# Opening of a two-layer transformer block: order of the modulation chunks, of the first weight loads and splits, and of the rows of h

## The chip, the cores and the metric

The kernel runs on one core of one Trainium2 chip, in one launch. The metric is the device time in microseconds (us); a median over the runs shown is compared. The core has five engines that work side by side and wait for one another by semaphores: PE (TensorE, matmuls), DVE (VectorE), ACT (ScalarE), POOL (GpSimd) and SP (SyncE), which here issues the DMA transfers. Each engine works through its own instructions in order. Line numbers such as L195 are lines of the kernel before.

## What is computed

The reference runs two layers over a sequence x of 512 tokens and a context of 256 tokens, both 1024 wide. Only the start of layer 0 matters here: the modulation vectors, the normalised and modulated input h, and its product with the first projection's weights. The filter of the long convolution is computed beside it.

```python
def _rms_norm(x, g):
    y = x32 * lax.rsqrt(jnp.mean(x32 * x32, axis=-1, keepdims=True) + EPS)
    return (y * _f32(g)).astype(x.dtype)

def _adaln(cond, w_mod, b_mod):
    mod = jax.nn.silu(cond) @ w_mod + b_mod
    return jnp.split(mod[:, None, :], 6, axis=-1)

def _modulate(h, shift, scale):
    return h * (1 + scale) + shift
...
        sh1, sc1, g1, sh2, sc2, g2 = _adaln(c, w_mod[i], b_mod[i])
        hx = _modulate(_rms_norm(x, norm1[i]), sh1, sc1)
...
def _fourier_hyena_mixer(h, w_in, w_out, ...):
    proj = h @ w_in
...
    h = jnp.sin(f * (z @ _f32(w1) + _f32(b1)))
    h = jnp.sin(f * (h @ _f32(w2) + _f32(b2)))
    h = jnp.sin(f * (h @ _f32(w3) + _f32(b3)))
    h = h @ _f32(w4)
```

## The kernel before

Activations lie with the 1024 features on the partitions, as eight row tiles of 128 features by 772 columns: 512 columns of x, two of padding, 256 of the context, two of padding. "Row d of h" is such a tile.

Products of full precision are made from split operands. A float32 value is kept as a high part in a reduced format and a low part, the rest. For a weight tile `wr` of 128 by 1024, ACT makes the high part `wh` (L98) and DVE the low part `wl` (L103); `wsplit` makes both, `wraw` only issues the load (L111). For a row of h, `a1` and `a2` (for x and for the context) call `scaled`, which lets DVE multiply by the norm and the scale A (L266) and ACT add the shift and write the high part `hh` (L267), and `low`, which lets DVE write the low part `hl` (L271). `mm3` then issues three matmuls for each product: `wh` by `hh` (L123), `wh` by `hl` (L124), `wl` by `hh` (L125). `proj_k` does that for one row k and one weight tile m, for the 512 and for the 260 columns: six matmuls, called a block here. `first(m, k)` is such a block, for the first three output tiles m of the projection and the eight rows k.

The modulation of layer 0 that h needs, shift and scale, is a product of the two conditions with 2048 columns of `w_mod`. It is made in four chunks of 512 columns. A chunk's weights are two loads of 1 MB (L180, `gemv_raw`) into one of three buffers `wm`. `gemv_pe` issues the chunk's matmuls (L189), the copy of their sums out of PSUM on ACT (L192), the turn, four products of a 128 by 128 piece of that copy with a selector of two columns (L195), which put the result on the partitions, and the add of the bias on DVE (L200). After the fourth chunk DVE makes A (L218), and then h can begin.

Between the chunks stand two other pieces. The norm's statistic takes squares on ACT (L233), sums them on PE (L234), copies the sums (L244), puts them on the partitions (L248), computes 1/sqrt by small DVE operations (the last is L141), spreads it over the partitions on PE (L256) and copies it to SBUF (L259); it runs once for x and once for the context. The three layers of the filter's small network each are a product (L359), a chain of DVE operations that reduces the argument of the sine (L333 to L342), and the sine on ACT (L343). The product of its result with w4 (L372) is the first thing that PE does after the blocks. Chunks, turns, statistics and layers share two PSUM buffers called `ms`.

The order of PE, DVE, ACT and SP in the opening is written out by hand: inside `manual_schedule` each engine works in the order in which the program calls. POOL's order, and all that comes after, is planned by the framework. Eight loads can be under way on SP's queue, since each of eight semaphores is used again only when its last load has landed.

Of the kernel before, what the change touches and what calls it, by code (L numbers as in the profile page):

```python
# [14 lines left out]
ALU = mybir.AluOpType  # L15
# [3 lines left out]
P = 128  # L19
D = 1024  # L20
KD = 8
# [12 lines left out]
def _columns():  # L34
    names = [("n1_0", 8), ("n1_1", 8), ("n2_0", 8), ("n2_1", 8), ("bm_0", 48), ("bm_1", 48)]
    names += [(f"fcw{i}{k}", NF) for i in range(2) for k in range(3)]
    names += [(f"fcb{i}", NF) for i in range(2)]
    names += [(f"hcw{k}", 12) for k in range(3)] + [("hcb", 12)]
    names += [("fb1", 1), ("fb2", 1), ("fb3", 1), ("ffr", 1)]
    names += [("qan", 2), ("kvan", 1), ("qg", 2), ("kg", 2), ("kpg", 1)]  # L40
    off, o = {}, 0
    for n, w in names:
        off[n] = (o, w)
        o += w
    return off, o


COLS, NCOLS = _columns()


class Builder:
# [130 lines left out]

    def gemv_pe(self, i, chunk, raw):

        nc = self.nc
        ps = self.ms()
        for kt in range(KD):
            q = kt % 4
            nc.tensor.matmul(ps[32 * q : 32 * q + 32, :], self.sT[:, kt, :], raw[:, 512 * kt : 512 * kt + 512],  # L189
                             start=kt < 4, stop=kt >= 4, tile_position=(0, 32 * q))  # L190
        g = self.t(self.S2, [P, 512], F32, "s2")
        nc.scalar.copy(g, ps)  # L192
        pc = self.ms()
        for b in range(4):
            nc.tensor.matmul(pc[:, 2 * b : 2 * b + 2], g[:, 128 * b : 128 * b + 128], self.sel, start=True, stop=True)  # L195
        sec, d0 = ((0, 0), (1, 0), (0, 4), (1, 4))[chunk]
        jt = 8 * sec + d0
        o = COLS[f"bm_{i}"][0] + jt
        bm = self.pcol[:, o : o + 4].rearrange("p (a o) -> p a o", o=1).to_broadcast([P, 4, 2])
        nc.vector.tensor_tensor(self.mod[i][:, jt : jt + 4, :], pc[:, 0:8].rearrange("p (a b) -> p a b", b=2), bm, op=ALU.add)  # L200

    def gemv_dve(self, i, jt, conds=(0, 1)):

# [255 lines left out]
    def mixer(self):  # L459
        nc, I = self.nc, self.I  # L460
# [19 lines left out]
        with self.tc.manual_schedule(engines={ENG.PE, ENG.DVE, ENG.SP, ENG.Activation}):  # L480
            layer = self.filter_mlp()
            for d in range(KD):
                nc.sync.dma_start(x[d][:, 0:512], I["xT"][d])
            wm = [self.gemv_raw(0)]
            for d in range(KD):
                nc.sync.dma_start(x[d][:, C0 : C0 + C], I["cxT"][d])
            wm.append(self.gemv_raw(1))
            nc.sync.dma_start(self.w4, I["w4"])
            wm.append(self.gemv_raw(2))
            pa = layer(0, None, 0)  # L490
            for d in range(KD):
                s1(d)
            h = layer(0, pa, 1)
            f1(True, 0)
            pa = layer(1, h, 0)
            f1(True, 1)
            h = layer(1, pa, 1)
            self.gemv_pe(0, 0, wm[0])
            wm.append(self.gemv_raw(3))
            for tt in (4, 5):  # L500
                dec[tt] = tp()
                nc.sync.dma_start(dec[tt], I["decay"][tt])
            win = [self.wraw(I["w_in"][m]) for m in range(3)]
            for d in range(KD):
                s2(d)
            f2(True, 0)
            pa = layer(2, h, 0)
            f2(True, 1)
            self.gemv_pe(0, 1, wm[1])
            h3 = layer(2, pa, 1)  # L510
            self.gemv_pe(0, 2, wm[2])
            self.gemv_pe(0, 3, wm[3])
            self.make_A(0, 0)
            self.close("wm")
            hp = self.pool("hp", side="right")
            for d in range(KD):
                hh.append(self.t(hp, [P, TW], F32R, f"hh{d}"))
                hl.append(self.t(hp, [P, TW], F32R, f"hl{d}"))
            self.zero_pads(hh + hl)

            def both(d, step):
                a1(d, step)
                return a2(d, step)


            ps3, wins = [self.mm() for _ in range(3)], []

            def first(m, k):
                self.proj_k(ps3[m], wins[m], hh, hl, k)

            both(0, 0)
            wins.append(self.wsplit(win[0]))
            both(1, 0)
            both(0, 1)
            first(0, 0)
            wins.append(self.wsplit(win[1]))
            both(2, 0)
            both(1, 1)
            first(0, 1)
            first(1, 0)  # L540
            first(1, 1)
            wins.append(self.wsplit(win[2]))
            both(3, 0)
            both(2, 1)
            first(0, 2)
            first(1, 2)
            first(2, 0)
            first(2, 1)
            first(2, 2)
            for d in range(4, KD + 1):  # L550
                if d < KD:
                    last_act = both(d, 0)
                last = both(d - 1, 1)
                for m in range(3):
                    first(m, d - 1)
        self.dbg("h0", hh, hl)


# [68 lines left out]
        def turn(i, f):  # L627
            pt = self.mm()
            for k in range(6):
                nc.tensor.transpose(pt[:, 128 * k : 128 * k + 128], f[:, 128 * k : 128 * k + 128], self.ident)  # L630
            src = pt[:, 0:768].rearrange("p (a b) -> p a b", b=128)
            w = slice(128 * i, 128 * i + 128)
            self.hi(uTh[:, :, w], src)
            self.lo(uTl[:, :, w], src, uTh[:, :, w])
# [96 lines left out]
        for src, b, c, n in ((I["cs128"], csh[:], csl[:], 256), (I["fcos"], flat(cth), flat(ctl), 1040), (I["fsin"], flat(sth), flat(stl), 1024)):  # L731
            for o in range(0, n, 520):
                m = min(520, n - o)
# [706 lines left out]
```

## Time and profile before

| | us |
|---|---|
| runs, median (3 runs) | 1829.6 |
| runs, lowest and highest | 1828.78 and 1830.51 |
| the profiled execution, its own time | 1830.64 |
| its span, first to last instruction | 1828.8 |
| PE busy in the span | 1706.3 (93%) |
| DVE busy | 1022.0 (56%) |
| ACT busy | 613.9 (34%) |
| POOL busy | 121.3 (7%) |

Durations in the profile come from one execution. Matmuls are pipelined, and their ends are modelled, so two that overlap add up to less than the sum of their records. A busy share over the whole span says little about the opening, which is 5% of it; it has to be read in its own stretch. The granted clock is the share of full speed at which PE was allowed to run; its mean over the span is 0.958. In the views of the trace an arrow in brackets names what ended the idle time before an instruction.

### The profile page before, as it was taken

The numbers are of one execution on the slowest core, as the hardware profiler recorded it, in microseconds if no ns is written. First come the engines' busy times: TensorE is split into PE (matmuls) and PEld (weight loads), VectorE is DVE, ScalarE is ACT, GpSimd is POOL, SyncE is SP. The second block draws the span as 40 slices with busy tenths as digits, with TensorE's granted clock in tenths as the row PEclk, the third lists the DMA queues.
The fourth block names the chain that finished last, engine by engine and source line by source line (L and its number), as shares of the span: only waits on it lengthen the run. The fifth ranks groups of instructions, "written<-read, shape, count | busy, mean of one in ns | idle before, by whom it ended". The sixth has DMA issues, their size and how long they took to land.

```text
span 1828.8 us, 21719 instructions
## 1 busy us (share of the span) xinstructions
PE 1706.3 (93%) x8742; PEld 1326.3 (73%) x8742; DVE 1022.0 (56%) x1662; ACT 613.9 (34%) x830; POOL 121.3 (7%) x202
## 2 busy tenths in 40 slices
PE   6889975799899999999999887899998999999999
PEld 2657864787688888888888556555554777888887
DVE  3486966864898435543434554665764554444443
ACT  3332222323323212222122434655663443223231
POOL 0052113310000000000000000110110000000000
PEclk7799987899999999999999998899999999999999
DMA  9032520352355234431312310000002323322322
GB/s 351 24 127 71 171 78 30 103 173 81 116 174 176 88 104 140 147 128 70 121 47 85 117 60 24 1 12 12 12 12 70 116 72 101 104 93 92 104 75 98
DMA packets 53249, 172.83 MB, mean 95 GB/s; under 512 B 6043, under 2 KB 8925, under 8 KB 52125
## 3 DMA queue, kind: packets, MB, share of 16 engines
q1 hardware_dynamic: 53149, 171.45, 27.4%
q8 instruction: 69, 1.13, 0.2%
q14 instruction: 31, 0.25, 0.0%
HBM read 167.23 MB, written 4.19 MB: 94 GB/s over the span
## 4 chain that ended last, share of the span: by engine, by line
PE 77%; DVE 11%; ACT 5%; POOL 3%; issue 3%; DMA 1%; POOLq 0%; SPq 0%; ACTq 0%; DVEq 0%
PE mm L123 21%; PE mm L124 20%; PE mm L125 20%; PE pv L1176 2%; PE ms L234 2%; PE z L1164 2%; DVE junk L210 2%; DVE wl L103 1%; DVE S L1154 1%; PE s L1130 1%; ACT S L1145 1%; PE s L123 1%; PE s L124 1%; PE s L125 1%; POOL s L388 1%
## 5 line engine op out<-in xcount | busy, mean ns | idle before, releaser
L123 PE MATMUL mm<-hh,wh 128*128 128x512 f32 (+2 forms) x1344 | 474.7, 356 | 7.0 <-ACT wh L98 3.4
L124 PE MATMUL mm<-hl,wh 128*128 128x512 f32 (+2 forms) x1344 | 473.9, 353 | 4.9 <-DVE hl L271 4.6
L125 PE MATMUL mm<-hh,wl 128*128 128x512 f32 (+2 forms) x1344 | 473.2, 353 | 1.3 <-DVE wl L103 1.3
L98 ACT ACTIVATE wh<-wr 128x1024 fp32r<-128x1024 f32 (+2 forms) x200 | 206.2, 1031 | 717.5 <-PE mm L124 646.5
L103 DVE TENSOR_TENSOR wl<-wr,wh 128x1024 fp32r<-128x1024 f32 (+2 forms) x200 | 243.6, 1219 | 287.3 <-ACT wh L98 279.6
L123 PEld LDWEIGHTS mm<-hh,wh 128*128 128x128 f32 x1344 | 254.4, 190 | 57.1 <-issue 12.0
L124 PEld LDWEIGHTS mm<-hl,wh 128*128 128x128 f32 x1344 | 255.0, 190 | 42.9 <-DVE hl L271 7.5
L125 PEld LDWEIGHTS mm<-hh,wl 128*128 128x128 f32 x1344 | 254.5, 190 | 38.4 <-issue 2.5
L123 PE MATMUL mm<-ah,wh 128*128 128x512 f32 (+1 forms) x528 | 187.8, 356 | 0.0
L124 PE MATMUL mm<-al,wh 128*128 128x512 f32 (+1 forms) x528 | 187.7, 356 | 0.0
L125 PE MATMUL mm<-ah,wl 128*128 128x512 f32 (+1 forms) x528 | 187.3, 355 | 0.0
L210 DVE SCALAR_TENSOR_TENSOR junk<-wr,sb 128x1024 bf16<-128x1024 f32 x128 | 159.3, 1244 | 36.7 <-DMA wr<-wmodT 36.6
L808 DVE SCALAR_TENSOR_TENSOR xr<-mm,mod,xr 128x512 f32<-128x512 f32 (+1 forms) x100 | 62.2, 642 | 204.3 <-PE mm L125 204.0
L123 PEld LDWEIGHTS mm<-ah,wh 128*128 128x128 f32 x528 | 99.1, 188 | 19.2 <-DVE xr L808 2.5
L124 PEld LDWEIGHTS mm<-al,wh 128*128 128x128 f32 x528 | 99.2, 188 | 15.3 <-issue 0.8
L125 PEld LDWEIGHTS mm<-ah,wl 128*128 128x128 f32 x528 | 99.2, 188 | 14.6
L1145 ACT ACTIVATE S<-s,rks 128x512 f32<-128x512 f32 x96 | 63.4, 688 | 44.3 <-PE s L125 43.4
L1154 DVE TENSOR_TENSOR S<-S,mb 128x1536 f32<-128x1536 f32 x32 | 54.8, 1752 | 20.7 <-POOL mb L1151 20.7
L845 ACT ACTIVATE fg<-fg 128x772 f32<-128x772 f32 (+1 forms) x44 | 32.6, 741 | 100.3 <-DVE fg L324 89.3
L1176 PE MATMUL pv<-S,V 128*64 128x512 f32 x192 | 58.9, 620 | 0.0
L1164 PE MATMUL z<-S,ones 128*32 128x512 f32 x192 | 42.7, 699 | 13.7 <-ACT S L1155 11.3
L1155 ACT ACTIVATE S<-S 128x1536 f32<-128x1536 f32 x32 | 47.1, 1481 | 18.0 <-DVE S L1154 18.0
(318 smaller groups left out, 2282.6 us busy)
## 6 DMA issues: line engine op xcount, KB each, us to landing
wr<-w_up SPq DMA_DIRECT2D x88, 512.0 KB, 3.3
wr<-wmodT SPq DMA_DIRECT2D x80, 512.0 KB, 3.3
wr<-w_dn SPq DMA_DIRECT2D x32, 512.0 KB, 3.2
wm<-wmod0a SPq DMA_DIRECT2D x8, 1024.0 KB, 9.6
wr<-w_in SPq DMA_DIRECT2D x16, 512.0 KB, 3.2
wr<-w_dn SPq DMA_DIRECT2D x20, 384.0 KB, 3.1
wr<-w_out SPq DMA_DIRECT2D x12, 512.0 KB, 3.2
wr<-w_o SPq DMA_DIRECT2D x12, 512.0 KB, 3.2
```

The lines of the kernel that those rows point to most:

```text
L98: self.nc.scalar.activation(dst, src, AF.Copy)
L103: (eng or self.nc.vector).tensor_tensor(dst, src, hi.bitcast(F32), op=ALU.subtract)
L123: mmul(out, wh, xh, start=start, stop=False)
L124: mmul(out, wh, xl, start=False, stop=False)
L125: mmul(out, wl, xh, start=False, stop=stop)
L210: nc.vector.scalar_tensor_tensor(junk, raw, 1.0, self.sb[:, j, :], op0=ALU.mult, op1=ALU.mult, accum_out=acc)
L808: nc.vector.scalar_tensor_tensor(x[m][:, a2:b2], ps[:, a2:b2], mod[:, 8 * sec + m, j : j + 1], x[m][:, a2:b2], op0=ALU.mult, op1=ALU.add)
L1145: nc.scalar.activation(S[j // 3][:, j % 3, :], ps, AF.Copy, scale=rs[:, 2 * j + a : 2 * j + a + 1])
L1154: v.tensor_tensor(s, s, mb3.to_broadcast([P, 3, T]), op=ALU.subtract)
L1155: nc.scalar.activation(s, s, AF.Exp)
L1164: nc.tensor.matmul(z[32 * g : 32 * g + 32, :], self.ones32, Ss[g // 2][(2 * k + g % 2) // 3][:, (2 * k + g % 2) % 3, :], start=k == 0, sto ...
L1176: nc.tensor.matmul(pv[64 * a : 64 * a + 64, :], V[:, k, 64 * h : 64 * h + 64], Ss[a][k // 3][:, k % 3, :], start=k == 0, stop=k == 5, tile ...
```

## The change

Nothing is added or removed; the same instructions are issued in another order.

- `gemv_pe` issues the chunk's matmuls and the copy, and returns a function `turn` that issues the turn and the add. The caller decides when.
- Turn 0 comes after the sums of the context's statistic (L234) instead of ahead of them. Chunk 1 comes after the statistic's L248, ahead of the filter's third layer and of the spread (L256) instead of behind both; its turn comes behind the spread. Chunks 2 and 3 stand directly behind one another, and turns 2 and 3 behind both.
- The three weight tiles of the projection are loaded directly behind the modulation's weights; w4 and two decay tiles, which were ahead of them, follow.
- The three tiles are split together: their `wh` on ACT behind the copy of chunk 3, their `wl` on DVE between the add of turn 2 and that of turn 3. Before, each split stood between two rows of h.
- The blocks are issued row by row: for each row its three blocks. Before, the first three rows came in an order that followed the splits.

```diff
     def gemv_pe(self, i, chunk, raw):
...
         nc.scalar.copy(g, ps)
-        pc = self.ms()
-        for b in range(4):
-            nc.tensor.matmul(pc[:, 2 * b : 2 * b + 2], g[:, 128 * b : 128 * b + 128], self.sel, start=True, stop=True)
...
+        def turn():
+            pc = self.ms()
+            for b in range(4):
+                nc.tensor.matmul(pc[:, 2 * b : 2 * b + 2], g[:, 128 * b : 128 * b + 128], self.sel, start=True, stop=True)
...
+        return turn
...
             wm = [self.gemv_raw(0)]
             for d in range(KD):
                 nc.sync.dma_start(x[d][:, C0 : C0 + C], I["cxT"][d])
-            wm.append(self.gemv_raw(1))
-            nc.sync.dma_start(self.w4, I["w4"])
-            wm.append(self.gemv_raw(2))
+            wm += [self.gemv_raw(1), self.gemv_raw(2)]
...
-            self.gemv_pe(0, 0, wm[0])
+            g0 = self.gemv_pe(0, 0, wm[0])
             wm.append(self.gemv_raw(3))
+            win = [self.wraw(I["w_in"][m]) for m in range(3)]
+            nc.sync.dma_start(self.w4, I["w4"])
             for tt in (4, 5):
                 dec[tt] = tp()
                 nc.sync.dma_start(dec[tt], I["decay"][tt])
-            win = [self.wraw(I["w_in"][m]) for m in range(3)]
             for d in range(KD):
                 s2(d)
+            g0()
             f2(True, 0)
+            g1 = self.gemv_pe(0, 1, wm[1])
             pa = layer(2, h, 0)
             f2(True, 1)
-            self.gemv_pe(0, 1, wm[1])
+            g1()
             h3 = layer(2, pa, 1)
-            self.gemv_pe(0, 2, wm[2])
-            self.gemv_pe(0, 3, wm[3])
+            g2 = self.gemv_pe(0, 2, wm[2])
+            g3 = self.gemv_pe(0, 3, wm[3])
+            g2()
+            wins = [self.wsplit(w) for w in win]
+            g3()
             self.make_A(0, 0)
...
-            both(0, 0)
-            wins.append(self.wsplit(win[0]))
-            both(1, 0)
-            both(0, 1)
-            first(0, 0)
-            wins.append(self.wsplit(win[1]))
...
-            for d in range(4, KD + 1):
+            for d in range(KD + 1):
                 if d < KD:
                     last_act = both(d, 0)
-                last = both(d - 1, 1)
-                for m in range(3):
-                    first(m, d - 1)
+                if d:
+                    last = both(d - 1, 1)
+                    for m in range(3):
+                        first(m, d - 1)
```

More of the change, by code (lines that the diff above doesn't have):

```diff
@@ L192, in gemv_pe @@
         nc.scalar.copy(g, ps)
-        pc = self.ms()
-        for b in range(4):
[L195 to L200, printed above, removed]
+        def turn():
+            pc = self.ms()
+            for b in range(4):
+                nc.tensor.matmul(pc[:, 2 * b : 2 * b + 2], g[:, 128 * b : 128 * b + 128], self.sel, start=True, stop=True)
+            sec, d0 = ((0, 0), (1, 0), (0, 4), (1, 4))[chunk]
+            jt = 8 * sec + d0
+            o = COLS[f"bm_{i}"][0] + jt
+            bm = self.pcol[:, o : o + 4].rearrange("p (a o) -> p a o", o=1).to_broadcast([P, 4, 2])
+            nc.vector.tensor_tensor(self.mod[i][:, jt : jt + 4, :], pc[:, 0:8].rearrange("p (a b) -> p a b", b=2), bm, op=ALU.add)
+        return turn
     def gemv_dve(self, i, jt, conds=(0, 1)):
@@ L523, in both @@
                 return a2(d, step)
-            ps3, wins = [self.mm() for _ in range(3)], []
+            ps3 = [self.mm() for _ in range(3)]
             def first(m, k):
                 self.proj_k(ps3[m], wins[m], hh, hl, k)
-            both(0, 0)
-            wins.append(self.wsplit(win[0]))
-            both(1, 0)
-            both(0, 1)
-            first(0, 0)
-            wins.append(self.wsplit(win[1]))
[L537 to L549, printed above, removed]
-            for d in range(4, KD + 1):
+            for d in range(KD + 1):
                 if d < KD:
                     last_act = both(d, 0)
-                last = both(d - 1, 1)
-                for m in range(3):
-                    first(m, d - 1)
+                if d:
+                    last = both(d - 1, 1)
+                    for m in range(3):
+                        first(m, d - 1)
         self.dbg("h0", hh, hl)
```

## The prediction

> **What bounds the kernel now.** I read the clock and the busy shares first, then the opening in order of time, then the DMA issues. The busy shares by stretch come first; I cut the span in steps of 3.41 us, because the clock in this trace changes only on such a grid (columns: busy us and instructions of PE, PEld, DVE, ACT, POOL; then granted clock, DMA share, GB/s).
>
> ```profile
> span 1828.8 us, 21719 instructions
> 21.57:24.98 3.41, 3.28 (x16) 0.39 (x8) 0.32 (x1) 0.59 (x2) 0.00 (x0) 0.50 0.99 417
> 24.98:28.40 3.42, 2.85 (x24) 1.81 (x24) 0.17 (x1) 2.98 (x9) 0.00 (x0) 1.00 1.04 435
> 28.40:31.81 3.41, 1.59 (x8) 0.74 (x6) 1.73 (x11) 0.37 (x1) 0.00 (x0) 1.00 1.02 423
> 31.81:35.22 3.41, 2.49 (x12) 1.33 (x16) 0.22 (x2) 0.37 (x1) 0.00 (x0) 0.50 1.00 416
> ...
> 45.46:48.88 3.42, 3.42 (x19) 1.99 (x23) 0.17 (x1) 0.00 (x0) 0.00 (x0) 0.50 0.02 10
> ...
> 65.94:69.36 3.42, 3.42 (x12) 2.95 (x12) 3.42 (x7) 1.86 (x4) 0.00 (x0) 0.50 0.23 77
> 69.36:72.77 3.41, 3.41 (x20) 2.98 (x20) 3.41 (x8) 1.51 (x3) 0.00 (x0) 1.00 0.02 7
> ```
>
> The clock rises after a filled step (21.57, 65.94) and falls after a thin one (28.40). From 31.81 to 69.36 PE runs at half clock, almost the whole stretch that the change reorders. The step 45.46 is filled and still brings no rise; 46.88 - 45.46 = 1.4 us of it is the turn (L195, two columns a matmul), so turns seem to count little.
>
> Now the opening in order of time: start, duration, engine, line, operation, count, and in brackets the idle time before it.
>
> ```profile
> 25.55 1.05 PE L195 MATMUL ms<-cst,s 128*128 128x2 f32 x8 [0.71 <-ACT s L192]
> 26.54 2.09 PE L234 MATMUL ms<-s,ones 128*32 128x256 f32 x16
> 29.09 0.61 PE L248 MATMUL ms<-cst,s 128*128 128x1 f32 x4 [0.46 <-ACT s L244]
> 29.56 0.89 PE L359 MATMUL ms<-s,fw 128*128 128x384 f32 x2
> 31.90 0.16 DVE L141 SCALAR_TENSOR_TENSOR rq_r<-rq_b,rq_r 128x2 f32<-128x2 f32 x1
> 32.21 1.19 PE L256 MATMUL ms<-cst,rq_r 128*128 128x128 f32 x4 [1.76 <-DVE rq_r L141]
> 33.49 0.37 ACT L259 COPY s<-ms 128x256 f32<-128x256 f32 x1 [4.46 <-PE ms L256]
> 33.92 3.64 PE L189 MATMUL ms<-wm,sT 128*32 128x512 f32 x16 [0.52 <-ACT s L259]
> 38.32 1.87 PE L195 MATMUL ms<-cst,s 128*128 128x2 f32 x8 [0.76 <-ACT s L192]
> 40.31 0.67 DVE L333 TENSOR_SCALAR s<-ms,pcol 128x384 f32<-128x384 f32 x1
> 40.44 3.64 PE L189 MATMUL ms<-wm,sT 128*32 128x512 f32 x16 [0.26 <-DVE mod L200]
> 44.03 0.52 ACT L343 ACTIVATE s<-s 128x384 f32<-128x384 f32 x1 [5.76 <-DVE s L342]
> 46.88 3.64 PE L189 MATMUL ms<-wm,sT 128*32 128x512 f32 x16
> 50.64 0.59 ACT L192 COPY s<-ms 128x512 f32<-128x512 f32 x1 [5.61 <-PE ms L189]
> 53.18 0.17 DVE L200 TENSOR_TENSOR mod<-ms,pcol 128x8 f32<-128x8 f32 x1 [6.03 <-PE ms L195]
> 53.66 1.15 DVE L266 SCALAR_TENSOR_TENSOR s<-x,A,s 128x512 f32<-128x512 f32 x2
> 55.47 1.04 ACT L98 ACTIVATE wh<-wr 128x1024 fp32r<-128x1024 f32 x1
> 56.54 1.23 DVE L103 TENSOR_TENSOR wl<-wr,wh 128x1024 fp32r<-128x1024 f32 x1 [1.74 <-ACT wh L98]
> 58.74 1.14 DVE L271 SCALAR_TENSOR_TENSOR hl<-s,mod,hh 128x512 fp32r<-128x512 f32 x2
> 59.54 0.79 PE L124 MATMUL mm<-hl,wh 128*128 128x512 f32 x1 [2.19 <-DVE hl L271]
> 63.56 0.80 PE L124 MATMUL mm<-hl,wh 128*128 128x512 f32 x1 [1.72 <-DVE hl L271]
> 65.23 0.63 PE L123 MATMUL mm<-hh,wh 128*128 128x512 f32 x1
> 65.73 1.14 DVE L266 SCALAR_TENSOR_TENSOR s<-x,A,s 128x512 f32<-128x512 f32 x2
> 67.16 0.63 PE L123 MATMUL mm<-hh,wh 128*128 128x512 f32 x1
> 67.84 1.14 DVE L266 SCALAR_TENSOR_TENSOR s<-x,A,s 128x512 f32<-128x512 f32 x2
> 78.74 0.39 PE L123 MATMUL mm<-hh,wh 128*128 128x512 f32 x1
> 79.79 0.39 PE L123 MATMUL mm<-hh,wh 128*128 128x512 f32 x1
> 90.43 3.70 PE L372 MATMUL mm<-w,s 64*128 64x512 f32 x8
> ```
>
> Until 53.66 the bound is a chain, not an engine: a chunk's matmuls (3.64), its copy (0.59), its turn (1.87), its add, and the next chunk queued behind it. From 53.66 to 63.56 it is DVE, which makes h and splits weights in turn while PE waits. From 63.56 PE runs without a gap to 90.43. One block (six matmuls, one weight tile by one row of h) takes 67.16 - 65.23 = 1.93 us at half clock and 79.79 - 78.74 = 1.05 at full; there are 24.
>
> **The change, part by part.** I follow the built order of the changed program; outside the opening it is the same on every engine.
>
> *Turn 0 deferred.* It now stands behind the context statistic, which ends at 26.54 + 2.09 = 28.63, so it ends near 29.65. L248 shares its buffer and waits for the add (0.17): it starts near 29.9 instead of 29.09, a loss of 0.8. The root is then done at 32.06 + 0.8 = 32.85.
>
> *Chunk 1 sooner.* It follows L248 after the 0.47 that L359 took (29.56 - 29.09): 30.35 instead of 33.92. Its time at full clock is in no row. Lower bound 3.64 / 2 = 1.82, upper 3.64; I take 3.64 x 1.05 / 1.93 = 2.0, the blocks' ratio, so it ends at 32.35. Third filter layer 0.9, to 33.2. L256 shares chunk 1's buffer, so it now also waits for that copy (0.59, to 33.0): nothing, L359 covers it. L256 at full clock 0.65 (1.19 by the same ratio), copy 0.37 and handovers: 34.3. Turn 1 1.05, add 0.2: chunk 2 starts near 35.6 instead of 40.44.
>
> *Chunks 2 and 3 back to back.* At full clock they end at 39.6; with one step of 3.41 us at half clock in between, 1.7 later. ACT holds the copy of chunk 2 behind the layer's sine, which takes 44.03 - 40.31 = 3.72 from its first operation: 39.3, its activation 39.85, copies to 40.4 and 41.0. So 41.0, or 42.0 with the cold step; I take 41.35, nearer the lower end, since the step filled by the two chunks raises the clock again.
>
> *Splits ahead of h.* wh of the first weight 1.04 after the copy, then three wl on DVE. Turn 3's add is queued behind all three, and who waits for it is A, and so all of h. Three wl cost 3 x 1.15 = 3.45 (1.23 less the overlap that paired operations show: 1.14 for two, 1.06 from pair to pair). Then add to first scaled row 53.66 - 53.18 = 0.48. Together 41.35 + 1.04 + 3.45 + 0.5 + handover = 46.4 instead of 53.66. The splits stand on the chain here, but in the old order the same three and the waits around them stood in the h rows. If the weights were late this cover would go; so the loads:
>
> ```profile
> 26.71 3.12 SPq L111 DMA_DIRECT2D wr<-w_in  x3
> wr<-w_in SPq DMA_DIRECT2D x1, 512.0 KB, 13.4
> ```
>
> The last of the three issues (by 29.83) lands 13.4 us on, so at 43.2 at the latest, with w4 and two decay tiles (1 MB together) ahead of it on SP's queue. Now they stand behind it; at the 417 GB/s of the first rows that is 2.5 us less, 40.7, and its split starts at 43.4. So the loads are hidden, and sooner loading is worth nothing by itself beyond keeping them hidden; w4 and decay move behind, to about 42, and their first reader is at 90.43 less the gain. SP's queue passes nothing else that is waited for.
>
> *h row by row.* From the first scaled row, two pairs of DVE operations (67.84 - 65.73 = 2.11) and the first low half (59.54 - 58.74 = 0.80) bring PE's first L124: 46.4 + 2.9 = 49.3. From there a row costs DVE 2.11 and PE three blocks, 3.15 to 5.8, so PE never waits again. Before, the same point was 63.56, with one block already done (1.05).
>
> *The sum.* A block costs 1.93 - 1.05 = 0.88 more at half clock, so each us until the clock rises costs 0.88 / 1.93 = 0.456. Before it rose 69.36 - 63.56 = 5.8 after the start of the run. On this trace's grid a run from 49.3 first fills the step 52.29 to 55.71: 6.4. Gain = 63.56 - 49.3 - 1.05 + 0.456 x (5.8 - 6.4) = 12.9. A rise after 3.4 to 6.8 would move that by +1.4 or -0.2. The profiled execution took 1830.64 around its span of 1828.8; that becomes 1817.7. The median of the runs, 1829.6, is 1.0 lower and becomes 1816.7.
>
> **Rivals.** *The clock is down in the chunks.* The step 28.40 to 31.81 will hold 0.2 of statistic, 1.46 of chunk 1, and turns; 1.59 (with a third of it L248) fell, 2.85 (with 1.05 turn) did not. Mine is between. And the grid may lie otherwise in another execution, so that chunk 0 does not fill a step. Then the rest of chunk 1 runs cold to 32.8, the layer (0.89 x 1.93 / 1.05 = 1.6) to 34.2, L256 to 35.4, copy to 35.9, turn 1 to 37.8: chunk 2 at 38.0. It ends at 41.6; the step 38.64 to 42.05 is filled, so chunk 3 speeds up and ends near 43.9. First scaled row 43.9 + 0.65 + 1.04 + 3.45 + 0.5 = 49.5, PE's run 52.4, mean rise after 5.1. Gain 63.56 - 52.4 - 1.05 + 0.3 = 10.4: 1819.2.
>
> *The clock never falls before h.* Copies to 41.0, first scaled row 46.05, run from 48.95, mean rise after 5.1: gain 63.56 - 48.95 - 1.05 + 0.3 = 13.9, so 1815.7. [...]
>
> *Nothing is left of it.* What follows would absorb the gain if it waited for something not moved. For it: 1738 us follow. Against: L372 at 90.43 follows PE's run without a gap, the order behind is the same, and loads are issued when buffers fall free. Price 12.9: 1829.6.
>
> *Slower: the clock stays at half through the whole PE run.* The row order begins after a long idle stretch, and if the rise failed to come, 24 blocks would cost 24 x 1.93 = 46.3: end 95.2 instead of 90.43, 4.8 lost, 1834.4. It decides from a rise later than 6.4 + 12.9 / 0.456 = 35 us after the start; before it needed 5.8.
>
> **How the numbers follow.** Forecast 0.46, clock down in the chunks 0.34, never falls 0.12, nothing left 0.05, slower 0.02, others 0.01. The range 1813.5 to 1821.5 takes in the first three with the rise at either bound and 2 us for the grid's other falls, later in the span; it leaves out about 0.15. What a measurement here can tell from no change is 0.2%, 3.7 us: faster 0.93 (the first three and a little of the rest), same 0.05, slower 0.02.
>
> **What would show it.** Right: chunk 2 near 35.6 with chunk 3 directly behind it; three wl in a row on DVE with the add behind them; first scaled row near 46.4; first L124 of row 0 near 49.3 and no PE gap until L372 near 77.5; the rest shifted unchanged. Wrong: a granted clock of 0.50 from 31.8 on (then 38.0, 49.5 and 52.4), wh waiting for a DMA, or PE gaps between the rows of h.

## The result, and the profile after

| | before | after |
|---|---|---|
| median of the runs on one chip (6 and 6) | 1829.19 us | 1816.31 us |
| lowest and highest | 1827.63 and 1831.63 | 1814.97 and 1820.35 |
| ratio after to before, 95% interval | | 0.9931 [0.9918, 0.9943] |
| span of the profiled execution | 1828.8 | 1813.4 |

The change made the kernel faster by 12.9 us. The forecast was 1816.7, from a gain of 12.9. The two traces show that the agreement is partly luck: in them the opening gained more, 16.4. The rest of the span took back 1.0 of it, and the other 2.5 lie between these two executions (1830.64 and 1815.18) and the medians.

First the busy shares of the kernel after, in steps of 3.41 us on the grid of its own clock (columns: start and end, length; busy us and instructions of PE, PEld, DVE, ACT, POOL; granted clock, DMA share, GB/s).

```profile
19.83:23.24 3.41, 3.25 (x16) 0.59 (x16) 1.65 (x4) 0.63 (x2) 0.00 (x0) 0.50 0.96 387
...
33.49:36.91 3.42, 3.16 (x30) 1.33 (x33) 2.60 (x7) 0.00 (x0) 0.00 (x0) 1.00 1.01 406
36.91:40.32 3.41, 2.14 (x20) 1.10 (x12) 1.08 (x3) 2.37 (x5) 1.01 (x32) 1.00 1.01 398
40.32:43.73 3.41, 1.84 (x8) 1.78 (x8) 3.31 (x3) 1.96 (x3) 0.00 (x0) 0.50 1.02 334
...
47.15:50.56 3.41, 3.41 (x11) 2.94 (x12) 3.41 (x7) 1.43 (x4) 0.00 (x0) 0.50 0.19 73
50.56:53.97 3.41, 3.41 (x21) 3.02 (x21) 3.41 (x8) 2.00 (x4) 0.00 (x0) 1.00 0.01 2
```

Chunk 0 runs at half clock, 3.51 for its 16 matmuls, as it did before (3.64, with the clock at 0.50 from 18.15 to 24.98). From 23.24 on the clock is full, through chunks 1 to 3, and it falls at 40.32, when only turn 3 and the wait for h are left. It is back at 50.56, 3.4 us after the first L124. Before, it was at half from 31.81 to 69.36.

Now the opening of the kernel after, in order of time (start, duration, engine, line, operation, count, idle time before). Lines are those of the changed kernel: chunk L190, its copy L193, turn L198, add L203, sine L348, scaled row L271, low half L276, product with w4 L377.

```profile
19.99 3.51 PE L190 MATMUL ms<-wm,sT 128*32 128x512 f32 x16 [0.68 <-ACT s L264]
27.22 1.05 PE L198 MATMUL ms<-cst,s 128*128 128x2 f32 x8
28.62 0.58 PE L253 MATMUL ms<-cst,s 128*128 128x1 f32 x4 [0.35 <-DVE mod L203]
29.13 1.93 PE L190 MATMUL ms<-wm,sT 128*32 128x512 f32 x16
33.04 1.05 PE L198 MATMUL ms<-cst,s 128*128 128x2 f32 x8 [0.52 <-ACT s L264]
34.36 3.64 PE L190 MATMUL ms<-wm,sT 128*32 128x512 f32 x32 [0.26 <-DVE mod L203]
37.95 0.52 ACT L348 ACTIVATE s<-s 128x384 f32<-128x384 f32 x1 [4.96 <-DVE s L347]
38.38 1.05 ACT L193 COPY s<-ms 128x512 f32<-128x512 f32 x2
39.32 2.96 ACT L98 ACTIVATE wh<-wr 128x1024 fp32r<-128x1024 f32 x3
40.40 1.84 PE L198 MATMUL ms<-cst,s 128*128 128x2 f32 x8 [0.35 <-ACT wh L98]
40.42 3.50 DVE L103 TENSOR_TENSOR wl<-wr,wh 128x1024 fp32r<-128x1024 f32 x3 [0.16 <-ACT wh L98]
43.83 0.16 DVE L203 TENSOR_TENSOR mod<-ms,pcol 128x8 f32<-128x8 f32 x1
44.23 2.21 DVE L271 SCALAR_TENSOR_TENSOR s<-x,A,s 128x512 f32<-128x512 f32 x4
45.79 0.80 PE L123 MATMUL mm<-hh,wh 128*128 128x512 f32 x1 [3.55 <-ACT hh L272]
47.15 0.80 PE L124 MATMUL mm<-hl,wh 128*128 128x512 f32 x1 [0.56 <-DVE hl L276]
73.99 3.70 PE L377 MATMUL mm<-w,s 64*128 64x512 f32 x8
```

Chunks 2 and 3 are one group of 32 matmuls in 3.64 us, the time that one chunk took before. The three wl stand in a row with the add behind them. The product with w4 starts 90.43 - 73.99 = 16.4 us sooner.

Last, everything behind that product as one stretch, in the kernel before, the kernel after, and a second profiled execution of the kernel after (experiment 4); each from its own view of busy shares.

```profile
90.43:1828.80 1738.37, 1637.69 (x8441) 1285.04 (x8440) 984.26 (x1570) 583.46 (x778) 120.15 (x166) 0.97 0.27 90
110.00:400.00 290.00, 240.76 (x1290) 200.29 (x1289) 218.01 (x355) 80.68 (x120) 76.19 (x132) 0.92 0.31 107
```

```profile
73.99:1813.40 1739.41, 1643.48 (x8441) 1289.77 (x8440) 982.92 (x1570) 583.64 (x778) 120.39 (x166) 0.97 0.26 90
110.00:400.00 290.00, 246.00 (x1301) 207.64 (x1300) 206.98 (x339) 79.80 (x118) 69.89 (x128) 0.90 0.30 103
```

```profile
74.11:1822.00 1747.89, 1652.75 (x8441) 1298.17 (x8440) 983.76 (x1570) 583.80 (x778) 120.46 (x166) 0.96 0.27 89
110.00:400.00 290.00, 246.10 (x1275) 208.34 (x1274) 205.55 (x336) 78.83 (x117) 69.81 (x128) 0.88 0.31 102
```

The number of instructions is the same (8441 on PE each time), but the stretch takes 1738.4, 1739.4 and 1747.9 us. The granted clock between 110 and 400, where PE often waits for DVE (33.1 us in the kernel before, 29.5 in the kernel after), is 0.92, 0.90 and 0.88. Two executions of one program differ there by 8.5 us, though their openings end within 0.1 us of each other.

### The profile page after: what moved, and what is told of

Same layout as the page of the kernel before. It is cut to its first block, busy times and chain, and to the rows that moved or that the text cites. A ratio compares the mean times of both kernels' runs of the same rounds, so it can differ in the third digit from the quotient of the medians.

```text
span 1813.4 us, 21720 instructions
## 1 busy us (share of the span) xinstructions
PE 1701.6 (94%) x8742; PEld 1326.4 (73%) x8742; DVE 1020.4 (56%) x1662; ACT 613.9 (34%) x830; POOL 121.6 (7%) x202
## 4 chain that ended last, share of the span: by engine, by line
PE 79%; DVE 9%; ACT 4%; POOL 3%; issue 2%; DMA 2%; SPq 0%; POOLq 0%; ACTq 0%; DVEq 0%
PE mm L123 22%; PE mm L124 21%; PE mm L125 21%; PE pv L1167 2%; PE z L1155 2%; PE ms L239 2%; DVE S L1145 1%; DVE wl L103 1%; PE s L1121 1%; ACT S L1136 1%; PE s L123 1%; DVE junk L215 1%; PE s L124 1%; PE s L125 1%; POOL s L393 1%
## 5 line engine op out<-in xcount | busy, mean ns | idle before, releaser
L123 PE MATMUL mm<-hh,wh 128*128 128x512 f32 (+2 forms) x1344 | 473.5, 355 | 7.2 <-ACT hh L272 6.9
L124 PE MATMUL mm<-hl,wh 128*128 128x512 f32 (+2 forms) x1344 | 473.4, 353 | 1.8 <-DVE hl L276 1.6
L123 PEld LDWEIGHTS mm<-hh,wh 128*128 128x128 f32 x1344 | 253.5, 189 | 57.1 <-issue 12.4
L124 PEld LDWEIGHTS mm<-hl,wh 128*128 128x128 f32 x1344 | 254.5, 189 | 39.6 <-DVE hl L276 4.1
L123 PE MATMUL mm<-ah,wh 128*128 128x512 f32 (+1 forms) x528 | 187.8, 356 | 0.0
L124 PE MATMUL mm<-al,wh 128*128 128x512 f32 (+1 forms) x528 | 187.7, 356 | 0.0
L123 PEld LDWEIGHTS mm<-ah,wh 128*128 128x128 f32 x528 | 99.1, 188 | 19.2 <-DVE xr L799 2.5
L124 PEld LDWEIGHTS mm<-al,wh 128*128 128x128 f32 x528 | 99.2, 188 | 15.3 <-issue 0.8
L1155 PE MATMUL z<-S,ones 128*32 128x512 f32 x192 | 42.6, 698 | 13.7 <-ACT S L1146 11.3
```

The lines of the kernel that those rows point to most:

```text
L123: mmul(out, wh, xh, start=start, stop=False)
L124: mmul(out, wh, xl, start=False, stop=False)
L1155: nc.tensor.matmul(z[32 * g : 32 * g + 32, :], self.ones32, Ss[g // 2][(2 * k + g % 2) // 3][:, (2 * k + g % 2) % 3, :], start=k == 0, sto ...
```

## The experiments

All times in us. "Row" is the start of the first scaled row of h, "L124" that of the first product with a low half, "w4" that of the product with w4 on PE, "rest" from there to the end of the span, all from one profiled execution each. Experiments 5 to 8 count the w4 product, in what was expected, from the semaphore ahead of it, 3.2 us sooner (70.8 for 73.99).

| kernel | chunks 2, 3 | row | L124 | w4 | rest | median (runs) | lowest to highest |
|---|---|---|---|---|---|---|---|
| before | 3.64 each | 53.66 | 59.54 | 90.43 | 1738.4 | 1829.2 (6) | 1827.6-1831.6 |
| after | 3.64 | 44.23 | 47.15 | 73.99 | 1739.4 | 1816.3 (6) | 1815.0-1820.4 |
| 1 chunks alone | 3.77 | 42.97 | 48.86 | 79.28 | 1741.1 | 1820.6 (6) | 1817.9-1822.2 |
| 2 splits and rows alone | 3.64 each | 55.66 | 58.58 | 85.55 | 1743.0 | 1828.3 (12) | 1821.6-1831.3 |
| 3 after, old loads | 3.64 | 45.16 | 48.08 | 74.73 | 1742.5 | 1819.2 (6) | 1817.2-1819.6 |
| 4 after, again | 3.64 | 43.23 | 46.15 | 74.11 | 1747.9 | 1817.8 (6) | 1814.3-1823.8 |
| 5 one wl ahead | 5.24 | 43.78 | 46.13 | 73.69 | 1744.9 | 1817.9 (6) | 1814.2-1821.4 |
| 6 as 5, sine later | 3.64 | 40.86 | 43.21 | 70.77 | 1738.2 | 1811.7 (4) | 1810.8-1812.2 |
| 7 as 6, wide filler | 5.34 | 45.17 | 47.51 | 75.12 | 1738.0 | 1812.8 (4) | 1811.9-1814.9 |
| 8 as 6, thin filler | 5.32 | 41.33 | 43.67 | 71.27 | 1744.7 | 1818.6 (5) | 1814.2-1820.0 |
| 9 before, filled | 1.92, 1.93 | 47.01 | 52.89 | 83.30 | 1741.2 | 1827.2 (12) | 1825.0-1831.9 |
| 10 after, late filler | 3.64 | 45.28 | 48.20 | 75.25 | 1739.7 | 1816.7 (6) | 1814.6-1823.7 |
| 11 as 6, again | 3.64 | 41.83 | 44.18 | 71.76 | 1742.7 | 1814.3 (6) | 1811.4-1820.0 |
| 12 as 6, late filler | 3.64 | 40.69 | 43.03 | 70.62 | 1745.0 | 1814.7 (6) | 1813.5-1817.5 |

The rest varies by 9.9 us between executions, though only experiments 10 and 12 add anything to it. What a change in the opening does is therefore read from the w4 column, and the medians only where they lie far apart.

### 1. The chunks alone

Loads, splits and rows stand as in the kernel before. Two places of the edit, here against the kernel after:

```diff
             g2()
-            wins = [self.wsplit(w) for w in win]
             g3()
...
+            both(0, 0)
+            wins.append(self.wsplit(win[0]))
...
```

> The kernel before with one part of the change alone: the chunks one behind another with deferred turns. Loads, splits and rows of h stand as before. Theory (the prediction's steps): the chunks carry most of the gain. No wl stands ahead of the add of turn 3, so the first scaled row comes 3.5 us sooner than the 44.23 of the changed kernel, near 40.7; the old order of splits and rows then needs the 63.56 - 53.66 = 9.9 us of before, so PE's unbroken run begins near 50.6 with one block done, some 2 us later than in the changed kernel: 1818 us (1816.5 to 1820). Rival: the splits and rows carry the gain, and the chunks only bring DVE's wait forward: 1826 us, with PE's run not before 57.

w4 comes at 79.28, 11.1 sooner than before: the chunks carry two thirds of the gain (1.0 of it is an earlier chunk 0, which in the kernel after is 1.2). Ratio to before 0.9945 [0.9928, 0.9962]. The median is above what was expected by 2.6, and outside the range given. Two lines of its opening in order of time show that the first scaled row was also later than expected (42.97, not 40.7):

```profile
40.63 1.84 PE L198 MATMUL ms<-cst,s 128*128 128x2 f32 x8 [0.35 <-DVE mod L203]
42.51 0.17 DVE L203 TENSOR_TENSOR mod<-ms,pcol 128x8 f32<-128x8 f32 x1 [2.02 <-PE ms L198]
```

Turn 3 runs at half clock to 42.47 (1.84, against 1.05 for turn 2), and the add starts then. So the three wl ahead of that add in the changed kernel, 3.50 us long, are partly hidden beside turn 3, which ends at 42.24 there; they delay the add by 43.83 - 42.24 = 1.6.

### 2. Splits ahead of h and rows in order, alone

The place that puts the splits ahead of the add of turn 3, against the kernel before; the blocks stand row by row as in the kernel after:

```diff
-            self.gemv_pe(0, 3, wm[3])
+            g3 = self.gemv_pe(0, 3, wm[3])
+            wins = [self.wsplit(w) for w in win]
+            g3()
```

> The kernel before with the other part alone: the three splits ahead of h, with the add of turn 3 behind them, and the blocks row by row. Chunks and turns otherwise as before, loads as before. Theory (the prediction's steps): three wl of 1.15 us push the first scaled row from 53.66 to about 56.2 to 57.2, the row order needs 2.9 us from there, so PE's run begins at 59.1 to 60.1 instead of 63.56 with one block (1.05) less done: gain 2.4 to 3.4, 1826 to 1827 us. The two parts' gains then add up to that of the whole change. Rival: the splits on the chain cost what the rows save, 1829 us. Second rival: this part carries the gain: 1819 us.

w4 comes at 85.55, 4.9 sooner; the two parts add up, 11.1 + 4.9 = 16.0 of 16.4. More than the 2.4 to 3.4 expected, since the first scaled row is 0.5 sooner and the clock rose at 62.25, 3.7 us after L124 (5.8 after the run began in the kernel before). The median, 1828.3, shows only 1.0 of it and lies nearer to the rival's 1829 than to the theory: 0.9988 [0.9976, 1.0000].

### 3. The loads in the old order

One place of the edit, against the kernel after; w4 also goes back ahead of the weights of chunk 2:

```diff
-            win = [self.wraw(I["w_in"][m]) for m in range(3)]
-            nc.sync.dma_start(self.w4, I["w4"])
             for tt in (4, 5):
...
+            win = [self.wraw(I["w_in"][m]) for m in range(3)]
```

> The changed kernel with the loads in the old order: w4 and the two decay tiles ahead of the projection's weights again. Theory of the prediction: the loads are hidden in either order, so the time stays at 1816.3 (within 0.7) and no wh waits for a DMA. Rival: the chunks end so much sooner that the old order of loads would be late. In the changed kernel the three tiles landed at 37.0 to 39.8 and were split from 39.3 on; in the kernel before they landed at 40.3 to 42.9. Then the first wh waits about 1 us and the third about 1.6, the first scaled row comes at 45 to 46, and the time is 1817.3 to 1818.

The rival's sign was right. In its opening, in order of time, each of the three wh waits for its load:

```profile
38.64 1.05 ACT L193 COPY s<-ms 128x512 f32<-128x512 f32 x2
39.98 1.06 ACT L98 ACTIVATE wh<-wr 128x1024 fp32r<-128x1024 f32 x1 [0.29 <-DMA wr<-w_in]
41.26 1.06 ACT L98 ACTIVATE wh<-wr 128x1024 fp32r<-128x1024 f32 x1 [0.22 <-DMA wr<-w_in]
42.53 1.06 ACT L98 ACTIVATE wh<-wr 128x1024 fp32r<-128x1024 f32 x1 [0.22 <-DMA wr<-w_in]
```

The waits are small, 0.73 in all, and from the end of the chunks to the first row it takes 45.16 - 38.26 = 6.9 instead of 44.23 - 38.00 = 6.2. So the sooner loads are worth 0.7 in this opening. The median, 1819.2, lies above both ranges given and is 1.4 above that of the kernel after in the same series (experiment 4); with the rest varying by more, no more than the 0.7 is shown.

### 4. The kernel after once more

Nothing is edited.

> The changed kernel as it is, once more, for its spread and for a second look at the clock. Theory: the grid on which the clock changes lies otherwise in each execution, so the fall comes at another place; executions in which the clock is down in the chunks are about 3 us longer (1819 to 1820.5) and stand beside those at 1815 to 1817. Rival: the one time of 1820.35 was a stray, every execution keeps full clock through the chunks, and all times lie between 1814.5 and 1817.5.

The spread is there, 1814.3 to 1823.8, wider than the rival's 1814.5 to 1817.5, but not for the reason that the theory gave. The profiled execution is the slowest, and its chunks ran at full clock (3.64 for the pair). Its opening ended as soon as the other's (74.11 and 73.99); the 8.5 us lie in the rest. The theory falls for this execution; the clock's other place in the grid shows as this:

```profile
34.97:38.39 3.42, 2.42 (x24) 0.78 (x16) 1.78 (x4) 1.44 (x4) 1.01 (x32) 1.00 1.02 404
38.39:41.80 3.41, 1.69 (x14) 1.54 (x14) 2.54 (x4) 2.89 (x4) 0.00 (x0) 1.00 1.05 396
41.80:45.21 3.41, 0.42 (x1) 0.29 (x1) 3.38 (x8) 1.20 (x3) 0.00 (x0) 0.50 1.02 399
```

It falls at 41.80, not 40.32, and rises at 52.04. The run of blocks starts 1.0 sooner but lies at half clock for 5.9 us instead of 3.4: 0.456 x 2.5 = 1.1, and w4 comes at the same time. That agrees with the price of a us at half clock.

### 5 to 8. One wl ahead of the add, the sine later, and two fillers

Experiment 5 leaves only the first wl ahead of the add of turn 3 (against the kernel after):

```diff
-            wins = [self.wsplit(w) for w in win]
...
+            for w in win:
...
+                self.hi(wh, w)
+                lows.append((wl, w, wh))
+            self.lo(*lows[0])
             g3()
...
+            both(0, 0)
+            both(0, 1)
+            self.lo(*lows[1])
+            both(1, 0)
+            self.lo(*lows[2])
```

> The changed kernel with only the first wl ahead of the add of turn 3; the second wl stands behind the low half of row 0 and the third behind the scaled row 1. Theory (the prediction's step): in the changed kernel the add of turn 3, and so all of h, is queued behind three wl. In its own trace turn 3 ends at 42.2 and its add starts at 43.83. With one wl ahead, first scaled row at 42.1 to 42.8 instead of 44.23, first L124 of row 0 at 43.9 to 44.6 instead of 47.15, the first product with w4 at 68.0 to 69.5 instead of 70.8, and 1813.5 to 1815.5 us. Rival: the splits between the rows make PE wait in turns as in the kernel before, the first product with w4 stays at 70 to 71, no gain.

None of the four times came as expected. In this execution the clock fell in the chunks (0.50 from 35.16 to 38.57), so that the pair took 5.24, the case that the prediction gave a chance of 0.34:

```profile
35.30 5.24 PE L190 MATMUL ms<-wm,sT 128*32 128x512 f32 x32 [0.26 <-DVE mod L203]
```

Of the eleven profiled executions with the new chunk order this came in three (5, 7 and 8), and cost 1.6 to 1.7. Counted from the end of the chunks, the wl do what was expected: the first row comes 43.78 - 40.54 = 3.2 later instead of 6.2 (0.7 of that because the copy of chunk 3 did not stand behind the sine), and w4 33.15 later instead of 35.99. From the chunks on the variant is 2.8 faster; the median, 1817.9, doesn't show it.

Experiment 6 also moves the sine on ACT behind row 0 (against experiment 5):

```diff
-        nc.scalar.activation(o[:, :n], a[:, :n], AF.Sin)
+        return lambda: nc.scalar.activation(o[:, :n], a[:, :n], AF.Sin)
...
             both(1, 0)
+            act3()
```

> As the run before it in this list, and the sine of the filter's third layer is issued on ACT behind row 0 of h instead of ahead of the copies of chunks 2 and 3. Theory: ACT holds both copies behind the sine (in the changed kernel it waits 4.96 us for DVE's part of it, and the copies start at 38.38, though chunk 2 is summed by 36.2). Without it the copies come at about 36.4 and 38.1, the add of turn 3 by 40.2 to 41, the first L124 of row 0 at 43.0 to 43.6, the first product with w4 near 67.5, 1812.5 to 1814.5 us. Rival: the chain is then held by something else that was hidden (the loads, landing at 37.0 to 39.8, or wl), and the first product with w4 comes no sooner than with the one change.

Its opening in order of time:

```profile
33.99 3.64 PE L190 MATMUL ms<-wm,sT 128*32 128x512 f32 x32 [0.26 <-DVE mod L203]
36.03 0.59 ACT L193 COPY s<-ms 128x512 f32<-128x512 f32 x1 [3.41 <-PE ms L190]
37.75 0.59 ACT L193 COPY s<-ms 128x512 f32<-128x512 f32 x1 [1.13 <-PE ms L190]
40.53 1.06 ACT L98 ACTIVATE wh<-wr 128x1024 fp32r<-128x1024 f32 x1 [0.23 <-DMA wr<-w_in]
40.86 1.15 DVE L271 SCALAR_TENSOR_TENSOR s<-x,A,s 128x512 f32<-128x512 f32 x2
43.21 0.79 PE L124 MATMUL mm<-hl,wh 128*128 128x512 f32 x1 [0.29 <-DVE hl L276]
70.77 3.70 PE L380 MATMUL mm<-w,s 64*128 64x512 f32 x8
```

Both copies follow their chunk at once; L124 and w4 came as expected (67.5 and the 3.2 make 70.7), and the median, 1811.7, below the range given. w4 comes 3.2 sooner than in the kernel after. The third wh now waits 0.23 for its load: the margin of the loads is used up in this execution. The time from the end of the chunks to w4 is 33.14, as in experiment 5, where the cold step had given the sine the time to get out of the way; so in these traces the sine costs only where the chunks run warm.

Experiments 7 and 8 add matmuls to the gap in which PE waits for h, whose result is overwritten (against experiment 6):

```diff
             g3()
...
+            for _ in range(3):
+                nc.tensor.matmul(ps3[2][:, 0:512], self.ident, x[0][:, 0:512], start=True, stop=True)
```

```diff
+            for _ in range(11):
+                nc.tensor.matmul(ps3[2][:, 0:2], x[0][:, 0:128], self.sel, start=True, stop=True)
```

> As the second of this list, with three matmuls of 512 columns behind turn 3, whose result nothing reads, in the gap in which PE waits for h. Theory (the clock counts how much of a step is filled): the step is filled, the clock stays at full, and PE's run of blocks does not begin at half clock; a block then costs 1.05 instead of 1.93 for the first 3.4 to 6.8 us, up to 1.6 to 3.1 us, of which DVE's splits between the rows, 1.15 each, take back about 1.5: first product with w4 at 65.5 to 67, 1811 to 1814 us. Rival: the clock falls after the chunks all the same, and the fillers run at half clock, 1.8 us each, and push the first block back by 2 us: first product with w4 at 69 or later.

> As the second of this list, with eleven matmuls of two columns (the turn's form) behind turn 3, whose result nothing reads: about the same busy time of PE, 2.9 us. Theory: turns count little for the clock, as the filled step 45.46 to 48.88 of the kernel before brought no rise; the clock falls after the chunks and rises 3.4 to 6.8 us after the blocks begin, as without fillers, and the time is that of the second of this list or longer, since the fillers run at half clock. Rival: busy time counts whatever the shape, the clock stays at full as with the wide ones, and the two runs with fillers agree.

The steps on the clock's grid, first with the wide filler, then with the thin one:

```profile
40.08:43.49 3.41, 3.06 (x31) 1.57 (x23) 0.17 (x2) 2.02 (x3) 1.01 (x32) 1.00 1.05 356
43.49:46.91 3.42, 3.42 (x15) 1.88 (x14) 2.86 (x7) 2.95 (x5) 0.00 (x0) 1.00 0.87 296
46.91:50.32 3.41, 3.12 (x15) 1.89 (x14) 3.41 (x6) 0.80 (x3) 0.00 (x0) 1.00 0.30 105
```

```profile
36.20:39.61 3.41, 3.06 (x30) 1.55 (x23) 0.22 (x2) 1.98 (x3) 1.01 (x32) 1.00 1.01 404
39.61:43.02 3.41, 3.41 (x31) 3.34 (x30) 2.80 (x7) 2.94 (x5) 0.00 (x0) 1.00 1.03 332
43.02:46.43 3.41, 3.31 (x9) 2.42 (x10) 3.41 (x6) 0.79 (x2) 0.00 (x0) 0.50 0.88 343
```

The step 43.49 to 46.91 is filled with wide matmuls (2.8 of it), and the clock stays up behind it. The step 39.61 to 43.02 is filled too (3.41 of 3.41), nearly all of it (3.3) with products of two columns, and the clock falls at its end. Busy time whatever the shape, the rival of experiment 8, doesn't explain this.

But the wide filler brought no time, and w4 missed what was expected; that its median, 1812.8, fell in the range given is luck. From the end of the chunks to w4 it takes 75.12 - 41.93 = 33.19, against 33.14 without filler and 33.19 with the thin one. At full clock PE catches up with DVE, which still has two wl between the rows. With the wide filler PE waits for the second of them, as a line of its opening in order of time shows:

```profile
51.24 0.49 PE L125 MATMUL mm<-hh,wl 128*128 128x512 f32 x1 [0.86 <-DVE wl L103]
```

With the wl between the rows, DVE holds the pace, and a lower clock costs nothing there.

### 9. The kernel before, with its gaps filled

```diff
         nc.scalar.copy(g, ps)
+        fill()
         pc = self.ms()
...
             pa = layer(2, h, 0)
+            fill(2)
...
+            fill(3)
             self.make_A(0, 0)
```

Each `fill` issues wide matmuls as in experiment 7: one ahead of each turn, two behind the third layer, three behind turn 3, nine in all.

> The kernel before, its order untouched, with ten matmuls of 512 columns whose result nothing reads, in the gaps in which PE waits: two behind the filter's third layer, one behind each chunk ahead of its turn, three behind turn 3, and so on. It tells the order of the change from the clock. Theory: a good part of the change's gain is that chunks that follow one another keep the clock up. With the steps filled, chunks 1 to 3 take 1.93 instead of 3.64 each and their turns 1.05 instead of 1.87; less the fillers' own 0.3 a chunk that is about 7 us: first scaled row at 46 to 47 instead of 53.66, the first product with w4 (90.43 before, 73.99 after the change) at 81 to 84, 1821 to 1824 us. Rival: the order alone carries the gain; the clock falls all the same or the fillers cost what they bring, the first product with w4 stays at 88 to 91, 1828 to 1831 us.

Its opening in order of time:

```profile
33.08 1.92 PE L189 MATMUL ms<-wm,sT 128*32 128x512 f32 x16 [0.52 <-ACT s L260]
37.11 1.92 PE L189 MATMUL ms<-wm,sT 128*32 128x512 f32 x16 [0.26 <-DVE mod L201]
42.73 1.93 PE L189 MATMUL ms<-wm,sT 128*32 128x512 f32 x16
47.01 1.15 DVE L267 SCALAR_TENSOR_TENSOR s<-x,A,s 128x512 f32<-128x512 f32 x2
```

With the order untouched, the clock stays up from 24.08 to 54.80, and w4 comes at 83.30, 7.1 sooner. The theory holds for the opening: in the order of before, a warm clock by itself is worth some 7 us, of the 16.4 that the whole change brought. The median fell by 2.1 only, to 1827.2 (0.9989 [0.9979, 0.9999]), which is above the range expected and nearer to the rival's.

### 10 and 12. A filler late in the span

Experiment 10 against the kernel after; 12 is the same edit against experiment 6:

```diff
             pt = self.mm()
+            for _ in range(5 if i == 3 else 0):
+                nc.tensor.matmul(pt[:, 0:512], self.ident, x0[0][:, 0:512], start=True, stop=True)
             for k in range(6):
```

> The changed kernel with five matmuls of 512 columns whose result nothing reads, ahead of the last six transposes of the mixer's first half, where PE waits 6.7 us for DVE. It asks where the gain of the opening is given back. Theory: by falls of the clock later in the span, which differ from execution to execution (the changed kernel had 58 us at half clock from 110 to 400 in one execution and 72 in another, with the opening the same to 0.1 us). One such fall, 10.2 us long, begins at 248.5 or 250 in both. Filled, it does not come: up to 0.456 x 10.2 = 4.6 us, of which DVE's chain leaves perhaps 2: 1813.5 to 1815.5 us, and a narrower spread. Rival: in that stretch DVE is the bound and the clock costs nothing: 1816 to 1818 us.

> The faster variant with the five matmuls ahead of the last six transposes as well. Theory: the two gains add up, 1809 to 1811.5 us. Rival: the filled step only moves the falls to other steps, and the time is that of the faster variant, 1811.5 to 1813.5 us.

The filler brought nothing in either, as the rivals said: 1816.7 against 1816.3 and 1817.8 without it, and 1814.7 against 1814.3 for the same kernel without the filler beside it. The number that the rival of experiment 12 gave, 1811.5 to 1813.5, was too low. In the trace of experiment 10, in order of time, the filler ends too soon:

```profile
246.70 4.45 PE L621 MATMUL mm<-x,cst 128*128 128x512 f32 x10
253.51 1.54 PE L623 MATMUL mm<-cst,tm 128*128 128x128 f32 x6 [2.35 <-DVE tm L614]
```

The clock fell all the same, at 253.44, and was down 6.8 us instead of 10.2. That a longer filler would pay is not shown. Five wide matmuls took 4.45 us, and PE then waited 2.35 more.

### 11. The faster variant again

> The faster variant (one wl ahead of the add of turn 3, the sine behind row 0) once more. Theory: its 1811.7 stands, 1811 to 1813 us, since its opening is 3.3 us shorter. Rival: its four times fell on a good grid; with the spread of the others its median is 1813.5 to 1815.

The rival's number: 1814.3. Its best runs (1811.4, 1811.5) repeat experiment 6, its others don't. All ten runs of 6 and 11 have a median of 1812.1, the twelve of the kernel after in both its series 1816.6; a resampling of these puts the ratio of the medians at 0.9975 [0.9959, 0.9992]. They come from different series, on different chips, so this is weaker than a comparison side by side. Against the kernel before in the same series, 6 and 11 stand at 0.9894 and 0.9917, the kernel after at 0.9931 and 0.9937. w4 at 70.77 and 71.76 against 73.99 and 74.11 says the same: 2 to 3 us better than the kernel after.

## Why the prediction was right

Point by point, with what the runs showed.

- *What bounds the opening.* Right. Shortening the chain gave 11.1 (experiment 1), the DVE part 4.9 (experiment 2), and they add up to nearly all of the 16.4.
- *Turn 0, chunk 1, turn 1.* Right to 0.1: chunk 0 began at 19.99 instead of 21.21 in this execution, 1.2 sooner, and chunk 2 at 34.36, which is 35.6 less 1.2. The change moves nothing that chunk 0 waits for, and its start differs anyway: in the other ten executions with the new order of chunks it lay between 19.93 and 21.35, and in the order of before (2 and 9) at 20.85 and 21.18.
- *Chunks 2 and 3.* The step of cold clock that was counted in by about a third did not come: copies done at 39.43 + 1.2 = 40.6 instead of 41.35, 0.7 less.
- *Splits ahead of h.* Copies to first row 4.8, predicted 5.05, 0.2 less. The price was real: with one wl ahead instead of three it takes 43.78 - 41.25 = 2.5 (the copy of chunk 3 in experiment 5 ends at 41.25).
- *Rows.* First row to L124 2.92, predicted 2.9, and then no gap in PE to the product with w4. Right.
- *The clock in the run of blocks.* Mis-sized: it rose after 3.4 us, not 6.4, worth 0.456 x 3.0 = 1.4. That is the lower bound that the prediction named (3.4 to 6.8); in experiment 4 it was 5.9.
- *Loads.* Hidden in the new order, as predicted. "Worth nothing by itself" was wrong by 0.7 (experiment 3): the chunks now end before the old order would have landed the tiles.

So the opening gained 12.9 + 1.2 + 0.9 + 1.4 = 16.4 in the profiled execution: the forecast's sum, the sooner start, the warm chunks with the shorter way to the first row (0.7 and 0.2), and the sooner rise. The start, the chunks and the rise differ from execution to execution.

The median gained 12.9 and not 16.4. In the two traces the rest took back 1.0 (1738.4 and 1739.4); beyond that the profiled execution of before lies 1.4 above its median and that of the kernel after 1.1 below. So the step that the record doesn't bear out is "the rest shifted unchanged": the rest is not one number. It took 1738.4 in the profiled execution of before, near the low end of the 1738.0 to 1747.9 of all fourteen. Time and clock go together: over the fourteen traces the rest grows by 0.26 us for each us at half clock in it (correlation 0.91). Over 45 runs of the kernel before, the span grows by 0.25 us for each us at half clock (correlation 0.90; half-clock time is twice the share missing from the granted clock, times the span), and over the twelve of the kernel after by 0.28 (0.96). By the medians the kernel after spends 136 us at half clock and the kernel before 153, 17 less, while the two profiled openings differ by 30.7 (44.4 and 13.7). The missing 13 us would be worth 13 x 0.28 = 3.6, which is the gap of 3.5.

Whether they lie in the rest of the kernel after, or whether the opening of before is often warmer than in its one profile, stays open: no second trace of the kernel before was taken. The record leans to the second reading. That one trace has only 110.8 us at half clock in its rest, where the fourteen have 103.9 to 141.8. And in twelve of the thirteen comparisons with it w4 gained more than the median did against the kernel before in the same series, by 3.6 on average over all thirteen, also where the kernel before only got fillers (7.1 and 2.1 in experiment 9).

Of the rivals, "the clock is down in the chunks" is real and came in 3 of 11 executions, for 1.6 to 1.7 us at the chunks and not the 2.5 that it was priced at, because chunk 1 stayed warm each time (1.92 to 1.93); 1.7 is what the forecast had put on one cold step. "The clock never falls before h" came in neither trace of the kernel after: the clock fell at 40.32 and 41.80, ahead of the first row. But its price, copies without a cold step, is nearer to what came than the forecast's. "Nothing is left of it" and "slower" fell with w4 at 73.99 and the median. (The sum of "slower" ends at 49.3 + 46.3 = 95.6 and not at 95.2, which changes nothing.) In the kernel after PE sat idle for 3.55 us ahead of the first L123, but the clock had fallen 1.9 before that gap began, behind a step with PE busy for 2.14 of 3.41 us (36.91 to 40.32). The grid on which the clock changes stood at 40.32 in one execution and at 41.80 in the other, 1.48 apart in steps of 3.41.

## What to carry to other kernels

Where short matmul groups alternate with copies and turns on one chain, put the groups behind one another and let the turns follow: here the chain got shorter and the clock stayed up (full from 23.24 to 40.32), and the clock alone was worth some 7 us in the order of before, where the whole change brought 16. Before a small operation that releases everything else, count what is queued ahead of it on its engine; one split ahead of it instead of three, and an activation that nobody waits for moved behind it, gave another 2 to 3 us here. And where the rest of a kernel moves by more than the edit is worth, read the edit from the point in the trace where its stretch ends.

## What the runs showed of the hardware

- The clock fell after a step in which PE was busy throughout, nearly all of it with products of two columns (experiment 8, 39.61 to 43.02). It stayed up after steps whose wide matmuls took 1.7 (47.97 to 51.38 in experiment 9) or about 2.0 of 3.41 us (34.97 to 38.39 in experiment 4), and it fell after steps in which they took 1.3 (the next one in experiment 9, 51.38 to 54.80) or 1.1 (36.91 to 40.32 in the kernel after). These are single steps.
- The same program took 8.5 us longer in one execution than in another behind an opening of equal length, with the clock lower: 141.8 us at half clock behind w4 in the slower, 117.6 in the quicker. At 0.28 us for each, these 24.2 account for some 6.8 of the 8.5.
- A lower clock cost nothing where DVE held the pace: 33.14 to 33.19 from the chunks to w4 whether PE's first blocks ran warm (experiment 7) or cold (5, 6 and 8).
